# The output projection's last pair of tiles finished one by one, and 1/rms with the mean's constant inside the square

## The chip, the cores and the metric

The kernel runs on one core of a Trainium2 chip, as one program. The metric is the device time of one execution in microseconds (us). Five engines work beside each other and meet at semaphores: TensorE (PE, matmuls and transposes; its weight loads are shown as PEld), VectorE (DVE), ScalarE (ACT), GpSimd (POOL) and SyncE (SP, which issues most of the DMAs). Each engine works off its own list of instructions in order.

## What is computed

The reference is a trunk of four layers over 512 latent tokens (x) and 256 context tokens (xc), 1024 wide, in float32. Layers 0 and 3 mix tokens with a chunked gated linear attention (GLA), layer 1 with windowed attention, layer 2 with a gated linear recurrence (RG-LRU, 1280 wide). Around each mixer stand a norm ahead, an output projection, a norm behind, and a residual:

```python
def rmsnorm(x, g):
    y = xf * lax.rsqrt(jnp.mean(xf * xf, axis=-1, keepdims=True) + EPS)
    return (y * g).astype(x.dtype)

for i in range(DEPTH):
    shift, scale, gate = jnp.split(s_lat @ w_mod[i] + b_mod[i], 3, axis=-1)
    h = rmsnorm(x, g_pre[i]) * (1.0 + scale[:, None, :]) + shift[:, None, :]
    ...
    y, yc = mixer(h, hc, ...)          # ends with (o * silu(z)) @ w_out
    x = x + gate[:, None, :] * rmsnorm(y, g_post[i])
    if ctx_out:                        # all layers but the last
        xc = xc + gate_c * rmsnorm(yc, g_post[i])
```

In a GLA layer each of the four heads' output has a norm of its own ahead of the gate: `o = merge_heads(rmsnorm(o, g_head))`.

## The kernel before

**Tiling.** Tokens lie in six tiles of 128: 0 to 3 are the latent ones, 4 and 5 the context. A float32 product is made of three passes, with both operands split in a rounded part and a rest (wh and wl for weights, Rh and Rl for the layer's input, transposed). `split` (L266 and L269) makes the two parts of a weight: ACT casts wh, then DVE, or for some parts POOL, subtracts to get wl. Weights come through a few buffers; `convert()` splits the next weight into the buffer of an old one, and so waits for that one's last reader.

**`finish` (L758)** is the output projection of a layer with all that stands behind it. Per token tile tt it has two column halves (ch) of 512, and each is summed over two halves of the contraction (kh). The first column half is done in a loop; the second by the generator `halves`, which takes a list of (kh, tt), does one product (L796, 12 matmuls) per step, and behind each product with kh = 1 runs `take` (ACT: Square of the result with a sum to ssq, L803; DVE: result times gate and weight, L804) and `post` (sum of the two halves' squares on DVE, L810, then 1/rms through `rstd_of`). `residual` (L816) adds to x and stores it, `square` is the next layer's sum of squares (ACT, L621, then `rstd_of`), `scale` multiplies by that 1/rms (L823), `norm` transposes one chunk of 256 columns of a tile pair (PE L638), applies the next layer's scale and shift (ACT L642) and splits into Rh and Rl (DVE L649 and L650). There are four chunks per pair; their results are the input of the next layer's first matmuls (L385 and others).

**Order.** In the three finishes that another layer follows, PE, ACT and DVE run in the order in which the code calls these steps (`manual_schedule`); POOL's order and the DMAs come from the scheduler. In the last part the pairs are (2, 3) for products and (0, 1) for the norm: the code there runs the products of tiles 2 and 3 and between them, as fillers, the norm's four chunks of tiles 0 and 1; then residuals, squares and scales of tiles 2 and 3, then the norm of pair (2, 3). The final finish (layer 3) has no norm behind it: it goes tile by tile.

**`rstd_of` (L611 to L616)** makes 1/rms on POOL: L614 multiplies the sum of squares by 1/n and adds EPS, L615 raises to -1/2. It serves rx (the pre-norm, 24 times), ry (the post-norm, 22 times) and ro (the GLA heads' norm, 20 times, 128x2).

**GLA.** In `chunk` (L1178 on) a pair of token tiles of one head is computed: PE L1188, ACT's squares L1190, DVE's multiplication by g_head L1191, `rstd_of`, DVE's scaling L1194 (two), then a transpose L1201. The scheduler orders these between heads: while the last chunks of one head end, the next head begins with `levels`, whose DVE operations are X (L1043) and then, level by level, X and Y (L1105); ACT copies Y to K (L1090), and PE's L1056 needs K.

Of the kernel before, what the change touches and what calls it, by code (L numbers as in the profile page):

```python
# [77 lines left out]
def body(ctx: ExitStack, tc: tile.TileContext, I, out, layers=(0, 1, 2, 3)):  # L78
# [532 lines left out]
    def rstd_of(pool, ss, n, name):  # L611
        w = ss.shape[1]
        r = pool.tile([P, w], F32, name=name, tag=name, bufs=4)
        G.tensor_scalar(r, ss, 1.0 / n, EPS, op0=ALU.mult, op1=ALU.add)  # L614
        G.tensor_tensor(r, r, nhalf.to_broadcast([P, w]), op=ALU.pow)  # L615
        return r  # L616

    def unit_rstd(pool, x, xn):

        ss = pool.tile([P, 1], F32, name="ssx", tag="ssx", bufs=4)  # L620
        S.activation(xn, x, AF.Square, accum_out=ss)  # L621
        return rstd_of(pool, ss, D, "rx")
# [135 lines left out]
    def finish(i, kc, extra, last, final, xsrc, xdst):  # L758
# [4 lines left out]
        with phase(f"fin{i}", 6, 0) as fp:  # L763
# [37 lines left out]
            def take(ch, tt, ps):  # L801
                c = slice(ch * 512, (ch + 1) * 512)
                S.activation(y[tt][:, c], ps, AF.Square, accum_out=ssq[tt][:, ch : ch + 1])  # L803
                V.tensor_tensor(y[tt][:, c], ps, gpt[:, 1 if tt >= 4 else 0, c], op=ALU.mult)  # L804
# [3 lines left out]
            def post(tt):  # L808
                s1 = fp.tile([P, 1], F32, name="s1", tag="s1", bufs=4)
                V.tensor_reduce(s1, ssq[tt], axis=AX.X, op=ALU.add)  # L810
                rs[tt] = rstd_of(fp, s1, D, "ry")
# [29 lines left out]
            def halves(*parts):  # L841

                ps = {}
                for kh, tt in parts:
                    if tt not in ps:
                        ps[tt] = mxt()
                    product(w[kh], kh, 1, tt, ps[tt])
                    yield
                    if kh:
                        take(1, tt, ps[tt])  # L850
                        post(tt)
# [32 lines left out]
            with tc.manual_schedule(engines={PE.engine, S.engine, V.engine}):  # L884
# [17 lines left out]
                h = halves((0, 2), (0, 3), (1, 2), (1, 3))  # L902
# [13 lines left out]
                step((0, 1), 0)  # L916
                next(h)
                norm((0, 1), 1)
                run(h)
                residual(2)  # L920
                norm((0, 1), 2)
                square(2)
                residual(3)
                norm((0, 1), 3)
                scale(2)
# [11 lines left out]
    def gla(i, a, ctx_out):  # L937
# [3 lines left out]
        with phase(f"gla{i}") as mp:  # L941
# [196 lines left out]
            def outputs(h, X, Y, A, v, tl):  # L1138
# [39 lines left out]
                def chunk(pr):  # L1178
# [10 lines left out]
                    for n in range(2):  # L1189
                        S.activation(on[:, n, :], ps[:, n, :], AF.Square, accum_out=ss[:, n : n + 1])  # L1190
                    V.tensor_tensor(on, ps, gh.unsqueeze(1).to_broadcast([P, 2, GDV]), op=ALU.mult)  # L1191
                    rs = rstd_of(mp, ss, GDV, "ro")
# [571 lines left out]
```

## Time and profile before

| | |
|---|---|
| median of 3 runs | 1525.08 us (1524.38 to 1532.94) |
| profiled execution, its own time | 1530.24 us |
| its span | 1528.5 us |
| mean granted TensorE clock | 0.983 |
| busy: PE | 1449.4 us, 95% |
| busy: DVE | 1013.6 us, 66% |
| busy: ACT | 786.9 us, 51% |
| busy: POOL | 190.5 us, 12% |

The profile page lists busy times over the whole span. Since PE is busy for most of it, the places to read are those where it waits. The three tails of `finish` lie at about 421 to 475, 848 to 897 and 1183 to 1224 us, the final one at the very end; the two GLA layers take the stretches from the start to about 421 and from 1224 to the end. The granted clock is the share of TensorE's full speed (2.4 GHz) that it was given; near 0.5 it ran at 1.2 GHz.

### The profile page before, as it was taken

The numbers are of one execution on the slowest core, as the hardware profiler recorded it, in microseconds if no ns is written. First come the engines' busy times: TensorE is split into PE (matmuls) and PEld (weight loads), VectorE is DVE, ScalarE is ACT, GpSimd is POOL, SyncE is SP. The second block draws the span as 40 slices with busy tenths as digits, with TensorE's granted clock in tenths as the row PEclk, the third lists the DMA queues.
The fourth block names the chain that finished last, engine by engine and source line by source line (L and its number), as shares of the span: only waits on it lengthen the run. The fifth ranks groups of instructions, "written<-read, shape, count | busy, mean of one in ns | idle before, by whom it ended". The sixth has DMA issues, their size and how long they took to land.

```text
span 1528.5 us, 29077 instructions
## 1 busy us (share of the span) xinstructions
PE 1449.4 (95%) x11691; PEld 1213.7 (79%) x11691; DVE 1013.6 (66%) x1913; ACT 786.9 (51%) x1543; POOL 190.5 (12%) x301
## 2 busy tenths in 40 slices
PE   5998899999999899999999999899999889999998
PEld 3877788888877777878888787788878778879886
DVE  5585647576264389787883568988962666766754
ACT  4644353524252357655662477878842555355242
POOL 2211101012122200010000210000011311101111
PEclk8999999999999999999999999999999999999999
DMA  9450514112573632122216624212251352121132
GB/s 304 138 149 18 170 56 143 56 33 70 206 235 128 183 94 70 43 66 56 56 45 226 216 82 150 82 49 70 66 188 50 102 158 88 33 59 56 60 110 84
DMA packets 153046, 162.35 MB, mean 106 GB/s; under 512 B 12418, under 2 KB 141968, under 8 KB 152912
## 3 DMA queue, kind: packets, MB, share of 16 engines
q1 hardware_dynamic: 147456, 146.56, 31.0%
q10 hardware_dynamic: 5456, 13.94, 2.5%
q8 instruction: 92, 1.51, 0.4%
q14 instruction: 42, 0.34, 0.1%
HBM read 138.44 MB, written 11.53 MB: 98 GB/s over the span
## 4 chain that ended last, share of the span: by engine, by line
PE 51%; DVE 10%; ACT 7%; DMA 5%; issue 2%; SPq 1%; POOL 1%; ACTq 0%; DVEq 0%; POOLq 0%
PE mxt L796 15%; PE pjt L395 9%; PE pjt L385 6%; PE pjt L1028 4%; PE mxt L1525 3%; PE mxt L1509 2%; DMA raw<-in_w_mod_dram 2%; PE mxt L524 2%; PE sct L1630 2%; PE mxt L1468 1%; PE mxt L1188 1%; PE mxt L1451 1%; DVE wl L269 1%; ACT wh L266 1%; PE mxt L638 1%
## 5 line engine op out<-in xcount | busy, mean ns | idle before, releaser
L385 PE MATMUL pjt<-Rh,wh 128*128 128x256 f32 (+1 forms) x592 | 198.6, 337 | 7.1 <-DVE Rh L649 4.6
L385 PE MATMUL pjt<-Rl,wh 128*128 128x256 f32 (+1 forms) x592 | 198.1, 336 | 2.1 <-DVE Rl L650 1.8
L385 PE MATMUL pjt<-Rh,wl 128*128 128x256 f32 (+1 forms) x592 | 197.2, 334 | 0.7 <-DVE wl L269 0.7
L269 DVE TENSOR_TENSOR wl<-raw,wh 128x1024 fp32r<-128x1024 f32 x105 | 128.4, 1231 | 56.8 <-ACT wh L266 56.4
L266 ACT CAST wh<-raw 128x1024 fp32r<-128x1024 f32 x118 | 122.0, 1053 | 80.8 <-PE mxt L796 33.0
L395 PE MATMUL pjt<-Rl,wh 128*128 128x512 f32 (+1 forms) x448 | 162.0, 362 | 0.0
L395 PE MATMUL pjt<-Rh,wh 128*128 128x512 f32 (+1 forms) x448 | 161.6, 361 | 0.0
L395 PE MATMUL pjt<-Rh,wl 128*128 128x512 f32 (+1 forms) x448 | 161.3, 360 | 0.0
L796 PE MATMUL mxt<-wh,Rh 128*128 128x512 f32 x352 | 138.9, 395 | 0.0
L796 PE MATMUL mxt<-wh,Rl 128*128 128x512 f32 x352 | 137.6, 391 | 0.8 <-DVE Rl L769 0.8
L796 PE MATMUL mxt<-wl,Rh 128*128 128x512 f32 x352 | 137.2, 390 | 0.0
L385 PEld LDWEIGHTS pjt<-Rh,wh 128*128 128x128 f32 x592 | 112.6, 191 | 19.7 <-DVE Rh L649 5.7
L385 PEld LDWEIGHTS pjt<-Rl,wh 128*128 128x128 f32 x592 | 112.7, 191 | 15.9 <-DVE Rl L650 4.1
L385 PEld LDWEIGHTS pjt<-Rh,wl 128*128 128x128 f32 x592 | 112.7, 191 | 12.5 <-DVE wl L269 1.2
L1028 PE MATMUL pjt<-wh,Rh 128*128 128x256 f32 x384 | 110.8, 289 | 1.9 <-ACT wh L266 1.9
L1028 PE MATMUL pjt<-wl,Rh 128*128 128x256 f32 x384 | 110.3, 287 | 1.1 <-DVE wl L269 1.1
L1028 PE MATMUL pjt<-wh,Rl 128*128 128x256 f32 x384 | 110.2, 287 | 0.0
L1487 ACT ACTIVATE pe<-mxt,mxs 128x256 f32<-128x256 f32 (+2 forms) x128 | 70.7, 556 | 54.0 <-DVE mxs L1479 53.1
L395 PEld LDWEIGHTS pjt<-Rh,wl 128*128 128x128 f32 x448 | 86.0, 192 | 9.2 <-issue 1.9
L395 PEld LDWEIGHTS pjt<-Rh,wh 128*128 128x128 f32 x448 | 86.3, 193 | 8.7 <-issue 1.2
L395 PEld LDWEIGHTS pjt<-Rl,wh 128*128 128x128 f32 x448 | 86.2, 193 | 8.5 <-issue 1.3
L1477 DVE TENSOR_REDUCE mxs<-mxt 128x1 f32<-128x256 f32 (+2 forms) x128 | 65.4, 518 | 24.1 <-PE mxt L1468 10.5
(297 smaller groups left out, 3458.1 us busy)
## 6 DMA issues: line engine op xcount, KB each, us to landing
rawp<-in_w_mod_dram SPq DMA_DIRECT2D x48, 512.0 KB, 5.7
raw<-in_w_mod_dram SPq DMA_DIRECT2D x48, 512.0 KB, 3.7
raw<-in_a_w_in_dram SPq DMA_DIRECT2D x32, 512.0 KB, 3.5
raw<-in_b_w_in_dram SPq DMA_DIRECT2D x20, 512.0 KB, 5.1
raw<-in_c_w_in_dram SPq DMA_DIRECT2D x20, 512.0 KB, 3.7
xd<-x SPq DMA_DIRECT2D x18, 512.0 KB
raw<-in_a_w_out_dram SPq DMA_DIRECT2D x16, 512.0 KB, 3.4
x<-xd ACTq DMA_DIRECT2D x16, 512.0 KB, 8.2
```

The costliest lines, as they stand in the source:

```text
L266: S.copy(h, x)
L269: e.tensor_tensor(l, x, h.bitcast(F32), op=ALU.subtract)
L385: PE.matmul(ps, w[u][:, k, c0 : c0 + P], R[v][:, k, t0 : t0 + n], start=(k == 0 and u + v == 0), stop=(k == KC - 1 and u == 1),)
L395: PE.matmul(ps, w[u][:, k, c0 : c0 + P], R[x][:, k, t0 : t0 + n], start=(k == 0 and u + x == 0), stop=(k == KC - 1 and u == 1),)
L524: PE.matmul(ps[32 * g : 32 * g + 32, 0:256], sT[:, k, :], r2[k // 4][:, k % 4, :], start=(n < 4), stop=(n >= 4), skip_group_check=True,)
L796: PE.matmul(ps, l[:, tt * P : (tt + 1) * P], r, start=(k == 0 and u + v == 0), stop=(k == kc - 1 and u == 1),)
L1028: PE.matmul(ps[:, n, :], R[u][:, k, tt * P : (tt + 1) * P], w[x][:, k, :], start=(k == 0 and u + x == 0), stop=(k == KC - 1 and u == 1),)
L1477: V.tensor_reduce(mxs[:, n : n + 1], u[e][:, :w], axis=AX.X, op=ALU.max)
L1487: S.activation(p[:, o : o + w], u[e][:, :w], AF.Exp, bias=nm, scale=0.125, accum_out=den[:, n : n + 1],)
L1509: PE.transpose(u[e][:, c * P : (c + 1) * P], ps[e][:, m * P : (m + 1) * P], ident)
L1525: PE.matmul(po[64 * e : 64 * e + 64, 0:P], v[:, keys[m], 64 * kv : 64 * kv + 64], pt[:, e, m * P : (m + 1) * P], start=(m == len(keys) - 1 ...
L1630: PE.matmul(ps[:, t0 : t0 + nn], wg[a][:, n, :], x[c][:, p0 : p0 + nn], start=(q == 0), stop=(q == 2),)
```

## The change

There are two parts. **The constants:** `rstd_of` no longer multiplies by 1/n. Instead the Square on ACT gets a scale of n to the power -1/2, so that the sum is already the mean. EPS is added on DVE by an operation of its own for rx and ro; for ry it is added in the operation that sums the two halves (a scalar_tensor_tensor in place of the reduction L810). POOL keeps the power alone, so it has 66 instructions fewer, and DVE 44 more. **The order:** in the finishes with a norm behind them, the products of the last pair run (0, 2), (1, 2), (0, 3), (1, 3) in place of (0, 2), (0, 3), (1, 2), (1, 3); residual, square and scale of tile 2 move ahead, and the norm's last chunks of pair (0, 1) stand ahead of tile 3's residual.

```diff
--- before.py
+++ after.py
@@ -608,18 +608,20 @@
             run(open_bg.pop())
 
 
-    def rstd_of(pool, ss, n, name):
+    def rstd_of(pool, ss, name, eps=True):
+
         w = ss.shape[1]
         r = pool.tile([P, w], F32, name=name, tag=name, bufs=4)
-        G.tensor_scalar(r, ss, 1.0 / n, EPS, op0=ALU.mult, op1=ALU.add)
-        G.tensor_tensor(r, r, nhalf.to_broadcast([P, w]), op=ALU.pow)
+        if eps:
+            V.tensor_scalar(r, ss, EPS, None, op0=ALU.add)
+        G.tensor_tensor(r, r if eps else ss, nhalf.to_broadcast([P, w]), op=ALU.pow)
         return r
 
     def unit_rstd(pool, x, xn):
 
         ss = pool.tile([P, 1], F32, name="ssx", tag="ssx", bufs=4)
-        S.activation(xn, x, AF.Square, accum_out=ss)
-        return rstd_of(pool, ss, D, "rx")
+        S.activation(xn, x, AF.Square, scale=D ** -0.5, accum_out=ss)
+        return rstd_of(pool, ss, "rx")
 
     def unit(pool, x, xn):
 
@@ -800,15 +802,15 @@
 
             def take(ch, tt, ps):
                 c = slice(ch * 512, (ch + 1) * 512)
-                S.activation(y[tt][:, c], ps, AF.Square, accum_out=ssq[tt][:, ch : ch + 1])
+                S.activation(y[tt][:, c], ps, AF.Square, scale=D ** -0.5, accum_out=ssq[tt][:, ch : ch + 1])
                 V.tensor_tensor(y[tt][:, c], ps, gpt[:, 1 if tt >= 4 else 0, c], op=ALU.mult)
 
             rs = {}
 
             def post(tt):
                 s1 = fp.tile([P, 1], F32, name="s1", tag="s1", bufs=4)
-                V.tensor_reduce(s1, ssq[tt], axis=AX.X, op=ALU.add)
-                rs[tt] = rstd_of(fp, s1, D, "ry")
+                V.scalar_tensor_tensor(s1, ssq[tt][:, 0:1], EPS, ssq[tt][:, 1:2], op0=ALU.add, op1=ALU.add)
+                rs[tt] = rstd_of(fp, s1, "ry", False)
 
             def residual(tt, parts=1):
                 for m in range(parts):
@@ -899,7 +901,7 @@
                 next(h, None)
                 step((4, 5), 1)
                 run(h)
-                h = halves((0, 2), (0, 3), (1, 2), (1, 3))
+                h = halves((0, 2), (1, 2), (0, 3), (1, 3))
                 step((4, 5), 2)
                 residual(0)
                 next(h)
@@ -914,15 +916,15 @@
                 convert()
                 next(h)
                 step((0, 1), 0)
+                residual(2)
                 next(h)
                 norm((0, 1), 1)
+                square(2)
                 run(h)
-                residual(2)
                 norm((0, 1), 2)
-                square(2)
+                scale(2)
+                norm((0, 1), 3)
                 residual(3)
-                norm((0, 1), 3)
-                scale(2)
                 square(3)
                 scale(3)
                 begin("ctx")
@@ -1187,9 +1189,9 @@
                         for m, (l, r) in enumerate(tm):
                             PE.matmul(ps[:, n, :], l, r, start=(m == 0), stop=(m == len(tm) - 1))
                     for n in range(2):
-                        S.activation(on[:, n, :], ps[:, n, :], AF.Square, accum_out=ss[:, n : n + 1])
+                        S.activation(on[:, n, :], ps[:, n, :], AF.Square, scale=GDV ** -0.5, accum_out=ss[:, n : n + 1])
                     V.tensor_tensor(on, ps, gh.unsqueeze(1).to_broadcast([P, 2, GDV]), op=ALU.mult)
-                    rs = rstd_of(mp, ss, GDV, "ro")
+                    rs = rstd_of(mp, ss, "ro")
                     for n in range(2):
                         V.tensor_scalar(on[:, n, :], on[:, n, :], rs[:, n : n + 1], None, op0=ALU.mult)
                     return on
```

What this moves is shown at three places. In the rows of after, the lines from L616 on are those of before plus 2 (L1196 is L1194 of before).

First, DVE in layer 3, where one head's last chunks meet the next head's first levels (on is the head's output, ro its 1/rms, X and Y the next head's scaled queries and keys). Before:

```order
L1191 TENSOR_TENSOR on<-mxt,gh 128x512
L1194 TENSOR_SCALAR on<-on,ro 128x256 x2
L1043 TENSOR_TENSOR X<-tmp,q 128x2x512
L1191 TENSOR_TENSOR on<-mxt,gh 128x512
L1194 TENSOR_SCALAR on<-on,ro 128x256 x2
L1105 TENSOR_TENSOR X<-X,tmp 128x256x2
L1105 TENSOR_TENSOR Y<-Y,tmp 128x384x2
```

after:

```order
L1193 TENSOR_TENSOR on<-mxt,gh 128x512
L616 TENSOR_SCALAR ro<-sso 128x2
L1196 TENSOR_SCALAR on<-on,ro 128x256 x2
L1045 TENSOR_TENSOR X<-tmp,q 128x2x512
L1193 TENSOR_TENSOR on<-mxt,gh 128x512
L616 TENSOR_SCALAR ro<-sso 128x2
L1196 TENSOR_SCALAR on<-on,ro 128x256 x2
L1107 TENSOR_TENSOR X<-X,tmp 128x256x2
L1107 TENSOR_TENSOR Y<-Y,tmp 128x384x2
```

The addition of EPS (L616) now stands behind each multiplication by g_head and ahead of the scaling that needs the power. This repeats for each head of both GLA layers.

Second, the tail of layer 1's finish, from the casts of `convert()` on (tiles 4 and 5 are done, so their y hold the norm's chunks: y_9209 and y_9213 before, y_9203 and y_9207 after; tiles 2 and 3 are y_9225 and y_9229 before, y_9219 and y_9223 after). ACT before:

```order
L266 CAST wh<-raw 128x1024 x2
L537 COPY mp<-mxt 128x256
L642 ACTIVATE y_9209<-mxt,modT 128x256 x2
L803 ACTIVATE y_9225,ssq_9226<-mxt 128x512
L642 ACTIVATE y_9213<-mxt,modT 128x256 x2
L803 ACTIVATE y_9229,ssq_9230<-mxt 128x512
L642 ACTIVATE y_9209<-mxt,modT 128x256 x2
L266 CAST wh<-raw 128x1024
L621 ACTIVATE y_9225,ssx<-x_9223 128x1024
L642 ACTIVATE y_9213<-mxt,modT 128x256 x2
L621 ACTIVATE y_9229,ssx<-x_9227 128x1024
L266 CAST wh<-raw 128x1024
```

and after:

```order
L266 CAST wh<-raw 128x1024 x2
L805 ACTIVATE y_9219,ssq_9220<-mxt 128x512
L537 COPY mp<-mxt 128x256
L644 ACTIVATE y_9203<-mxt,modT 128x256 x2
L644 ACTIVATE y_9207<-mxt,modT 128x256 x2
L623 ACTIVATE y_9219,ssx<-x_9217 128x1024
L805 ACTIVATE y_9223,ssq_9224<-mxt 128x512
L644 ACTIVATE y_9203<-mxt,modT 128x256 x2
L644 ACTIVATE y_9207<-mxt,modT 128x256 x2
L266 CAST wh<-raw 128x1024
L623 ACTIVATE y_9223,ssx<-x_9221 128x1024
```

Tile 2's take (the first L803, now L805) stands directly behind the casts, its square ahead of tile 3's take, and both last chunks of the norm ahead of tile 3's square. DVE there, from tile 3's sum on (s_9850 before, s_9846 after), before:

```order
L810 TENSOR_REDUCE s_9850<-ssq_9230 128x1
L816 SCALAR_TENSOR_TENSOR x_9223<-y_9225,ry,x_9223 128x1024
L649 CAST Rh<-y_9209 128x2x256
L269 TENSOR_TENSOR wl<-raw,wh 128x1024
L650 TENSOR_TENSOR Rl<-y_9209,Rh 128x2x256
L816 SCALAR_TENSOR_TENSOR x_9227<-y_9229,ry,x_9227 128x1024
L649 CAST Rh<-y_9213 128x2x256
L650 TENSOR_TENSOR Rl<-y_9213,Rh 128x2x256
L823 TENSOR_SCALAR y_9225<-x_9223,rx 128x1024
L823 TENSOR_SCALAR y_9229<-x_9227,rx 128x1024
```

and after:

```order
L812 SCALAR_TENSOR_TENSOR s_9846<-ssq_9224 128x1
L651 CAST Rh<-y_9203 128x2x256
L652 TENSOR_TENSOR Rl<-y_9203,Rh 128x2x256
L825 TENSOR_SCALAR y_9219<-x_9217,rx 128x1024
L651 CAST Rh<-y_9207 128x2x256
L269 TENSOR_TENSOR wl<-raw,wh 128x1024
L652 TENSOR_TENSOR Rl<-y_9207,Rh 128x2x256
L818 SCALAR_TENSOR_TENSOR x_9221<-y_9223,ry,x_9221 128x1024
L616 TENSOR_SCALAR rx<-ssx 128x1
L825 TENSOR_SCALAR y_9223<-x_9221,rx 128x1024
```

Tile 2's scale and both chunks of the norm, with the L269 between the two halves of the last, now stand ahead of tile 3's residual.

Third, POOL in the tail of layer 0's finish (s_4929 and s_4957 before, s_4882 and s_4959 after, are the sums of tiles 2 and 3). Before:

```order
L614 TENSOR_SCALAR ry<-s_4929 128x1
L615 TENSOR_TENSOR ry<-ry,nhalf 128x1
L614 TENSOR_SCALAR ry<-s_4957 128x1
L615 TENSOR_TENSOR ry<-ry,nhalf 128x1
L269 TENSOR_TENSOR wl<-raw,wh 128x1024
L614 TENSOR_SCALAR rx<-ssx 128x1
L615 TENSOR_TENSOR rx<-rx,nhalf 128x1
L614 TENSOR_SCALAR rx<-ssx 128x1
L615 TENSOR_TENSOR rx<-rx,nhalf 128x1
```

and after:

```order
L617 TENSOR_TENSOR ry<-s_4882,nhalf 128x1
L617 TENSOR_TENSOR rx<-rx,nhalf 128x1
L617 TENSOR_TENSOR ry<-s_4959,nhalf 128x1
L269 TENSOR_TENSOR wl<-raw,wh 128x1024
L617 TENSOR_TENSOR rx<-rx,nhalf 128x1
```

The power for tile 2's rx has moved ahead of tile 3's ry and of POOL's L269, and the power for tile 3's rx stands behind that L269 still.

## Rows read from the trace of the kernel before

**Rows 1.** The page: its first line, and busy time by engine (share, instructions)
```profile
span 1528.5 us, 29077 instructions
...
PE 1449.4 (95%) x11691; PEld 1213.7 (79%) x11691; DVE 1013.6 (66%) x1913; ACT 786.9 (51%) x1543; POOL 190.5 (12%) x301
```

**Rows 2.** PE's waits: line waited for, us in total, times, longest
```profile
PE mxt L524 <- DMA rawp<-in_w_mod_dram: 2.6, 1, 2.6
PE sct L1056 <- ACT K L1090: 6.4, 7, 1.1
PE pjt L385 <- DVE Rh L649: 4.6, 4, 2.0
PE mxt L638 <- DVE y L823: 1.7, 2, 1.0
PE mxt L1201 <- DVE on L1194: 0.4, 1, 0.4
```

**Rows 3.** The timeline, last tile: start, us, line, operation, [idle before <-releaser]
```profile
1522.79 0.14 DVE L810 TENSOR_REDUCE s<-ssq 128x1 f32<-128x2 f32 x1
1523.02 0.19 POOL L614 TENSOR_SCALAR ry<-s 128x1 f32<-128x1 f32 x1 [4.61 <-DVE s L810]
1523.30 0.55 POOL L615 TENSOR_TENSOR ry<-ry,nhalf 128x1 f32<-128x1 f32 x1
```

**Rows 4.** The timeline of a chunk handover in layer 3
```profile
1303.66 0.69 DVE L1191 TENSOR_TENSOR on<-mxt,gh 128x512 f32<-128x512 f32 x1 [2.28 <-ACT on L1190]
1303.99 0.70 POOL L615 TENSOR_TENSOR ro<-ro,nhalf 128x2 f32<-128x2 f32 x1
1304.72 0.62 DVE L1194 TENSOR_SCALAR on<-on,ro 128x256 f32<-128x256 f32 x2 [0.37 <-POOL ro L615]
1306.39 0.69 DVE L1191 TENSOR_TENSOR on<-mxt,gh 128x512 f32<-128x512 f32 x1
1307.35 0.62 DVE L1194 TENSOR_SCALAR on<-on,ro 128x256 f32<-128x256 f32 x2 [0.27 <-POOL ro L615]
1311.00 0.67 PE L1056 MATMUL sct<-X,K 128*32 128x32 f32 x32 [0.91 <-ACT K L1090]
```

**Rows 5.** The timeline of a handover in layer 0, DVE
```profile
226.31 0.69 DVE L1191 TENSOR_TENSOR on<-mxt,gh 128x512 f32<-128x512 f32 x1 [0.76 <-ACT on L1190]
226.92 0.41 DVE L492 SCALAR_TENSOR_TENSOR OG<-OG,gz 128x256 f32<-128x256 f32 x1
229.70 1.76 DVE L1043 TENSOR_TENSOR X<-tmp,q 128x1536 f32<-128x1536 f32 x1 [1.72 <-PE mxt L1188]
```

**Rows 6.** The chain that ended last, layer 1's tail: start, us, what
```profile
871.03 2.95 PE mxt L796 x12
```

**Rows 7.** The timeline of layer 1's tail, ACT and DVE
```profile
871.89 2.00 ACT L266 CAST wh<-raw 128x1024 fp32r<-128x1024 f32 x2
888.81 0.75 DVE L823 TENSOR_SCALAR y<-x,rx 128x1024 f32<-128x1024 f32 x1 [0.71 <-POOL rx L615]
```

**Rows 8.** Groups by line in layer 1's tail: busy us, mean ns, idle
```profile
L816 DVE SCALAR_TENSOR_TENSOR x<-y,ry,x 128x1024 f32<-128x1024 f32 x2 | 2.6, 1277 | 0.0
```

**Rows 9.** The timeline of layer 0's tail: POOL, DVE, PE
```profile
458.53 2.60 POOL L269 TENSOR_TENSOR wl<-raw,wh 128x1024 fp32r<-128x1024 f32 x1
458.80 3.41 DVE L816 SCALAR_TENSOR_TENSOR x<-y,ry,x 128x1024 f32<-128x1024 f32 x1
464.66 0.75 DVE L823 TENSOR_SCALAR y<-x,rx 128x1024 f32<-128x1024 f32 x1 [0.72 <-POOL rx L615]
466.50 1.04 PE L638 MATMUL mxt<-ident,y 128*128 128x128 f32 x4
```

**Rows 10.** The timeline of layer 2's tail, PE
```profile
1216.71 3.46 PE L638 MATMUL mxt<-ident,y 128*128 128x128 f32 x15 [0.70 <-DVE y L823]
```

**Rows 11.** Busy time by stretch: us, each engine busy (x), PEclk, DMA, GB/s
```profile
464.00:467.00 3.00, 3.00 (x23) 1.40 (x22) 1.17 (x4) 0.36 (x1) 0.55 (x1) 0.50 0.46 185
1215.00:1222.00 7.00, 6.30 (x31) 5.92 (x31) 3.96 (x8) 3.85 (x8) 0.79 (x2) 0.52 0.14 47
```

## The prediction

> **What bounds the kernel now.** I read the page's head first: 1528.5 us of span, TensorE (PE) busy for 95% of it [rows 1]. The profiled run took 1530.24 us, 1.7 over its span and 5.2 over the median of 1525.08; the sum below is a difference, and I apply it to the median. With PE at 95% a change can only gain or lose where PE waits, so the second view is PE's list of waits [rows 2]. Four of the rows shown touch this change most. The largest is 6.4 us in seven waits for K, the copy that ScalarE (ACT) makes in a GLA layer from Y, which VectorE (DVE) has scaled. Two belong to the tails of the three projections with a following norm: 4.6 us for Rh of the next layer's input and 1.7 us for the scaled tile y. The last, 0.4 us, is for the head norm's output at the end of layer 0. These waits together are 13.1 us, which is the most that it could take away at full clock. The third view is the timeline at those places, to see which engine ends last there.
>
> **The last tile of the program.** Its chain is the reduction L810, POOL's scale-and-add L614, POOL's power L615, the residual [rows 3]. L614 starts 0.23 after L810's start, L615 0.28 after L614. The change puts EPS into the operation at L810's place and drops L614; that scalar_tensor_tensor is not shown here at 128x1, so its price is bounded by nothing and by a rise from 0.14 to POOL's 0.19, and I take 0.14. **-0.3 us**, certain to be on the path, since nothing follows but two stores.
>
> **The head norm (ro), 20 times.** Here L614 goes off POOL too, but to DVE, as an operation of its own behind L1191. Before, POOL adds EPS while DVE multiplies: L1191 starts at 1303.66, the power at 1303.99 already, and the scale L1194 follows at 1304.72, 1.06 after L1191's start [rows 4]. After, the addition stands behind L1191 in DVE's order (the order rows of layer 3 above). L1191 gives way to the next operation 0.61 after its start [rows 5]; the addition, which no row shows on DVE, is bounded by nothing and by 0.19, the time on POOL [rows 3], and I take 0.15 (L810 on two columns is 0.14); the hop to POOL is 0.09 (0.23 less 0.14), the power 0.70, the hop back 0.03 (1303.99 + 0.70 to 1304.72). That makes 1.58 in place of 1.06, **+0.52**. For the second chunk, where the spacing is 0.96 (1306.39 to 1307.35), it is +0.62. Queued behind L1194 on DVE are the multiplications X and Y of L1105, behind Y ACT's copy K, and behind K PE's L1056, which at 1311.00 had waited 0.91 for it [rows 4]. So both delays add up on the path: 1.1 us for each of three heads in layer 3. The order of PE gives one more values matmul ahead of that wait, so I take 0.9 of it: **+2.7**.
>
> In layer 0 there are three chunks. Before the first L1043 DVE was idle for 1.72 us, waiting for PE [rows 5], which swallows the first two delays (1.0 to 1.2 together). The third stands behind L1043 and is not covered: +0.6 for two heads; in the third head DVE's order has an L490 between L1191 and L1194, which covers part, and I take 0.2 (between nothing and 0.6). With +0.3 at the layer's end, where PE already waits 0.4 for L1194 [rows 2], that is **+1.7**. The GLA layers together: +4.4, between 0 (if PE's extra work covers every delay) and +6 (no cover, every chunk's 0.52 to 0.62).
>
> A rule on which engine should do this speaks for the change, and the rows say otherwise. The Trainium skill, page "GPSIMD Engine Reference", section "4.1 Engine selection", sends elementwise work on a tile to VectorE and advises against GpSimd. By that alone the swap of 0.28 on POOL for 0.24 on DVE would cost the GLA layers nothing, and the sum would be +2.4 in place of +6.8; the spacing of 1.06 contradicts it here, because POOL's addition ran beside L1191 and DVE's cannot.
>
> **The three tails.** The products now go (0,2), (1,2), (0,3), (1,3), so tile 2 can be normed one product sooner, and the norm's chunks of tiles 0 and 1 no longer stand behind tile 3's residual. But the reordering also keeps the first weight half (kh = 0) in use until the third product instead of the second, and convert()'s two casts L266, which write the buffer of that half, must wait for its last reader.
>
> Layer 1: the third product ends at 871.03 + 2.95 = 873.98 [rows 6], the casts started at 871.89 [rows 7], so they move by 2.1. In ACT's order tile 2's take stands behind them and has to wait too, so its earlier product buys nothing. On DVE two L269 wait for the casts, then come tile 2's take, three modT operations, chunk 0 and residual 2. Later another L269 stands between L649 and L650 of chunk 3, waiting for a cast that stands behind chunk 3 on ACT, and the last residual (1.28 each [rows 8]) stands behind it. Walking these queues through with the durations of the tail before, tile 3's L823 starts at about 890.9, where it started at 888.81 [rows 7]. PE had no wait of size there, and has four matmuls of the next layer more to do early, so it now waits: **+2.0** (0 to +2.1).
>
> Layer 0: the last residual took 3.41 in place of 1.28, because POOL ran its L269 for 2.60 from 458.53 [rows 8, 9], and PE waited 2.0 for Rh behind it [rows 2]. After, Rh's last chunk stands ahead of the residual, and that wait goes. But POOL's L269, its cast late by the buffer, becomes ready at about 459.1, ahead of the power for rx3 in POOL's order, and falls on DVE's L650 of chunk 3; the residual behind it ends at about 463.5, L823 starts at 465.6 where it was 464.66, and ends at 466.4. PE came to tile 3's transposes at 466.50 before [rows 9], since the work ahead of them ran at a granted clock of 0.50 [rows 11]. So the idle time moves from ahead of that work to behind it: **0** (-2.5 if L269 misses DVE, +1.7 if the low clock then falls on more matmuls).
>
> Layer 2: the same way, POOL's L269 and the memset stand in other gaps; tile 3's L823 ends at about 1217.4 in place of 1216.7, where PE already waited 0.7 for it [rows 10]: **+0.7** (-1.7 to +0.7).
>
> **The first norm and the squares.** The six rx of the first norm take the same swap. They lie beside the first modulation products, which wait 2.6 us for a weight from DMA [rows 2]; that hides them, and without this cover they would cost up to six times 0.52, 3.1 us. The scale in ACT's squares replaces no instruction and adds none, so I cost it at nothing; it is bounded by the spread of ACT's own rows, which show no price for a scale.
>
> **The sum.** -0.3 + 2.7 + 1.7 + 2.0 + 0 + 0.7 = +6.8, that is 1525.1 + 6.8 = 1531.9 us.
>
> **The rivals.**
> Tails pay (chance 0.2). If POOL's L269 of layers 0 and 2 misses DVE's two-input operations, layer 0 gives -2.5, layer 2 -1.7 and layer 1 still +0.9: with +4.4 and -0.3 the sum is +0.8, 1525.9 us. For it: only two of the tail's DVE operations were hit before. Against: the operations that take both inputs from SBUF are now closer together.
>
> The clock stays up (faster; chance 0.15). After the long idle stretches PE ran at 0.50 in 464 to 467 and at 0.52 in 1215 to 1222 [rows 11]; at full clock the work in them would take half, so 1.5 to 1.7 and 3.4 us were lost. If the earlier chunk 3 and tile 2 keep PE fed so that it never falls, those 5 us come back, and with them the 6.3 us of waits for Rh and y [rows 2]: -11.3, and with the GLA layers' +4.4, the -0.3 and half of layer 1's 2.0 some 1519 us. It decides as soon as the tails save more than the GLA layers' 4.4 and layer 1's 2.0, over 6.4 of those 11.3. Against it: by the queues tile 3's L823 is not earlier in any tail.
>
> More clock lost (slower; chance 0.1). The waits for K grow from 0.91 to near 2, and the idle time that led to the 0.50 stretch was of 2.0 [rows 2, 11]. If the clock falls behind three to six of them, at 1.7 each, 1537 to 1542 us. Against: in layer 3 PE has matmuls between these waits.
>
> The change does nothing in the GLA layers (chance 0.1): PE's extra work hides the ro delay, and +2.4 is left, 1527.5 us.
>
> **Chances.** The forecast itself has 0.45, with its own range of 1529 to 1535. The range that should hold 8 in 10 takes in tails that pay and GLA layers that don't, most of the clock rival and the lower half of the slower one: 1520 to 1538. A measurement of this kernel tells about 1% from no change, 15.3 us; of these cases only the ends of the two clock rivals reach below 1509.8 or above 1540.3, so faster 0.02, the same 0.94, slower 0.04.
>
> **What would show it.** In the new trace: the power for ro starting only after L1191's end and L1194 1.6 after L1191's start (the GLA term); PE's waits for K longer by about 0.9 in layer 3; the casts L266 at 874.0 in layer 1's tail and tile 3's L823 near 891; POOL's L269 of layer 0 beside a DVE operation of over 2 us. The prediction is wrong if L1194 follows L1191 as before, if tile 3's L823 comes 2 us earlier in layers 0 and 2, or if the two stretches at half clock are gone.

## The result, and the profile after

The changed kernel took 1539.64 us in the median (1533.69 to 1616.59, 12 runs), the kernel before, run beside it, 1526.68 (1524.38 to 1533.47, 12 runs). The ratio is 1.0079 with a 95% interval of 1.0063 to 1.0095: **slower by 0.8%, some 12 us** (9.6 to 14.5). The forecast was slower by 6.8 us, with 1538.0 as the upper end of the range. The direction was right, the size was too small, and the time lies above the range. (1616.59 is one execution at a granted clock of 0.844, which the ratio leaves out.)

The page of the changed kernel, its first line and busy times [rows 1]:

```profile
span 1531.9 us, 29031 instructions
...
PE 1445.7 (94%) x11691; PEld 1209.0 (79%) x11691; DVE 1019.5 (67%) x1957; ACT 787.0 (51%) x1543; POOL 167.0 (11%) x235
```

The work is the same but for POOL, 23.5 us and 66 instructions less, and DVE, 5.9 us and 44 instructions more. PE's waits (line waited for, us in total, times, longest), as in [rows 2]:

```profile
PE mxt L1203 <- DVE on L1196: 7.2, 15, 0.7
PE sct L1058 <- ACT K L1092: 6.2, 7, 1.1
PE mxt L640 <- DVE y L825: 4.9, 4, 2.4
PE pjt L385 <- DVE Rl L652: 4.4, 10, 1.8
PE pjt L385 <- DVE Rh L651: 2.3, 1, 2.3
```

The row for K, which the forecast said would grow, is where it was: 6.2 us in 7, after 6.4 in 7. What is new is the first row: PE waits 7.2 us in 15 for the head norm's output, where it was 0.4 in one. The wait for y has gone from 1.7 to 4.9, that for Rh from 4.6 to 2.3, and that for Rl from 1.8 to 4.4 us.

The handover in layer 3 that [rows 4] showed, in the timeline after (start, us, engine, line):

```profile
1302.83 0.69 DVE L1193 TENSOR_TENSOR on<-mxt,gh 128x512 f32<-128x512 f32 x1 [2.27 <-ACT on L1192]
1303.44 0.16 DVE L616 TENSOR_SCALAR ro<-sso 128x2 f32<-128x2 f32 x1
1303.67 0.70 POOL L617 TENSOR_TENSOR ro<-ro,nhalf 128x2 f32<-128x2 f32 x1 [30.85 <-DVE ro L616]
1304.41 0.62 DVE L1196 TENSOR_SCALAR on<-on,ro 128x256 f32<-128x256 f32 x2 [0.82 <-POOL ro L617]
1304.91 0.63 PE L1203 MATMUL mxt<-ident,on 128*128 128x128 f32 x4 [0.55 <-DVE on L1196]
1306.08 0.68 DVE L1193 TENSOR_TENSOR on<-mxt,gh 128x512 f32<-128x512 f32 x1
1307.64 0.61 DVE L1196 TENSOR_SCALAR on<-on,ro 128x256 f32<-128x256 f32 x2 [0.81 <-POOL ro L617]
1308.14 0.63 PE L1203 MATMUL mxt<-ident,on 128*128 128x128 f32 x4 [0.20 <-DVE on L1196]
1311.32 0.73 PE L1058 MATMUL sct<-X,K 128*32 128x32 f32 x32 [0.94 <-ACT K L1092]
```

The addition starts 0.61 after L1193, the power 0.23 later, and L1196 1.58 after L1193: the spacing that was forecast, to the hundredth. The second chunk has 1.56 in place of 0.96. PE now waits for this at its own next instruction, the transposes L1203 of the same chunk, before it ever comes to K.

The last tile [rows 3]: the spacing from the sum to the power is 0.22 in place of 0.51.

```profile
1526.52 0.15 DVE L812 SCALAR_TENSOR_TENSOR s<-ssq 128x1 f32<-128x1 f32 x1
1526.74 0.55 POOL L617 TENSOR_TENSOR ry<-s,nhalf 128x1 f32<-128x1 f32 x1 [4.89 <-DVE s L812]
1527.33 1.42 DVE L818 SCALAR_TENSOR_TENSOR x<-y,ry,x 128x512 f32<-128x512 f32 x2 [0.66 <-POOL ry L617]
```

### Where the time went, stage by stage

All 11691 matmuls are in both programs, so a stage can be priced by how much later the same matmul starts (the shift). One trace of before isn't enough for this. The execution shown ahead of the prediction took 1530.24 us, 1.9 to 3.6 over the median of before in any of these comparisons; a second trace of it (the first experiment below) took 1527.11. The table has the shift gained within each stage, from the traces (us, median over the matmuls at the stage's end, less that at its start):

| stage | forecast | against the second trace | against the one shown before |
|---|---|---|---|
| GLA, layer 0, first handover (140 to 158) | +0.6 | +1.1 | +1.1 |
| GLA, layer 0, the others and the end (222 to 425) | +1.1 | +2.0 | +3.1 |
| tail of layer 0 (to 500) | 0 | +1.3 | -0.7 |
| tail of layer 1 (850 to 900) | +2.0 | +1.9 | +1.9 |
| tail of layer 2 (1185 to 1252) | +0.7 | +1.4 | +1.1 |
| GLA, layer 3 (1294 to the last tile) | +2.7 | +4.5 | +4.6 |
| last tile | -0.3 | -0.3 | -0.3 |
| sum of these | +6.8 | +11.9 | +10.8 |
| all the rest | 0 | -5.3 | -7.4 |

Both sums, 11.9 and 10.8, lie in the measured interval of 9.6 to 14.5. The rest differs by several us from execution to execution, and the traced execution of the changed kernel took 1533.69, the least of its twelve, so the difference of two traces' spans (+6.6 and +3.4) says little here.

Not all rows are equally firm. The steps in the GLA layers are the same against either trace: 1.1, 1.0 and 0.7 us at the three handovers of layer 0 and 0.8 at its end, 1.2, 1.3 and 1.3 at those of layer 3 and 0.7 at its end, 8.1 in all. (The table's 7.6 is less by 0.5 which the second trace itself loses behind the second handover.) Layer 1's tail is as steady. Layer 0's tail has +1.0 by 473, the end of its transposes, against the second trace. Behind layer 2's tail the shift against the second trace falls by 1.2 again at 1255, where that trace waits 1.1 us for a weight's DMA and the changed kernel does not.

### The profile page after: what moved, and what is told of

The parts are those of the page before. It is cut to its first block, busy times and chain, and to the rows that moved or that the text cites. A ratio compares the mean times of both kernels' runs of the same rounds, so it can differ in the third digit from the quotient of the medians.

```text
span 1531.9 us, 29031 instructions
## 1 busy us (share of the span) xinstructions
PE 1445.7 (94%) x11691; PEld 1209.0 (79%) x11691; DVE 1019.5 (67%) x1957; ACT 787.0 (51%) x1543; POOL 167.0 (11%) x235
## 4 chain that ended last, share of the span: by engine, by line
PE 48%; DVE 13%; ACT 7%; DMA 4%; issue 3%; POOL 1%; SPq 1%; ACTq 0%; DVEq 0%; POOLq 0%
PE mxt L798 14%; PE pjt L395 9%; PE pjt L385 6%; PE pjt L1030 4%; PE mxt L1527 2%; PE mxt L1511 2%; PE sct L1632 2%; DVE wl L269 1%; PE mxt L1470 1%; PE mxt L524 1%; ACT wh L266 1%; PE mxt L1453 1%; DMA raw<-in_w_mod_dram 1%; DMA bb<-in_b_mod_dram 1%; PE mxt L1162 1%
## 5 line engine op out<-in xcount | busy, mean ns | idle before, releaser
L269 DVE TENSOR_TENSOR wl<-raw,wh 128x1024 fp32r<-128x1024 f32 x105 | 128.0, 1230 | 56.5 <-ACT wh L266 56.0
L806 DVE TENSOR_TENSOR y<-mxt,gpt 128x512 f32<-128x512 f32 x44 | 30.3, 689 | 75.6 <-ACT y L805 75.4
```

Of the source, the lines that this page charges most:

```text
L269: e.tensor_tensor(l, x, h.bitcast(F32), op=ALU.subtract)
```

## The experiments

### A second trace of the kernel before

No edit.

> The kernel before once more, for a second trace of it. The profiled execution shown of it took 1530.24 us, 2 to 3.5 over its median, and shows stretches at half clock at 464 and 536 us and none near 1290, where the changed kernel and all four variants have one. Theory A (which stretches fall to half clock differs from execution to execution; the tail of layer 0 is about 1 us slower with the change than with an undisturbed clock): the new trace lacks the stretch at 464 or 536 or both, or has the one near 1290. Rival E (those stretches belong to the kernel): the same stretches again.

1527.11 us. Busy time by stretch in layer 0's tail (stretch, its length, then PE, PEld, DVE, ACT, POOL busy in us with counts, PEclk, DMA share, GB/s), and near 1290:

```profile
464.00:467.00 3.00, 3.00 (x34) 2.13 (x33) 1.40 (x5) 0.95 (x3) 0.85 (x2) 1.00 0.59 228
1288.00:1291.00 3.00, 3.00 (x12) 2.66 (x11) 2.43 (x4) 0.58 (x2) 0.00 (x0) 0.51 0.66 193
```

PE's first transposes of tile 3 in layer 0's tail, in the timeline:

```profile
465.65 0.68 PE L638 MATMUL mxt<-ident,y 128*128 128x128 f32 x4
```

The clock is 1.00 here, where the trace shown had 0.50 in 464 to 467 [rows 11], and PE comes to the transposes without a wait, 29.1 us after the pair's first product in place of 30.7 [rows 9]. The stretch near 1290, which the shown trace lacks, is there in this one, at 0.50. Theory A holds: those stretches belong to an execution, not to the kernel. Over all fourteen traces, the stretch near 464 stands in four: in the one shown and in three of the variants below.

### The two halves of the change apart

The first has the diff's hunk in the order of the finish alone, with `rstd_of` and its callers as before:

> The order of the finish as in the change, the constants as before (POOL does L614 and L615 for rx, ry and ro). Theory A (most of the loss is the head norm's EPS behind L1191 on DVE, about 7 us by the shift of PE's matmuls between the two traces; the tails cost about 2): +1 to +4 us, 1528 to 1531, PE's waits for the head norm's output near the 0.4 us of before. Rival B (the loss comes from the tails, the constants cost nothing): +9 to +13, 1536 to 1540. Rival C (a lower granted clock in more runs, from either part): the time tells nothing apart, but the mean granted clock of the runs lies under that of before's.

1535.18 us against 1528.31, ratio 1.0046 (1.0028 to 1.0064), +4 to +10. PE's wait for the head norm's output is back at 0.4, the shift in its GLA layers grows by no more than 0.1 at any handover, and the tails' shifts in its trace are +2.5, +2.0 and +1.4. (Of the +2.5, 1.1 stands by 473; the rest lies behind the tail, where PE waits 2.7 us for a weight's DMA in place of 1.3.) That is more than theory A allowed for and less than rival B. Rival C falls: the mean granted clock of the runs is 0.985, as that of before's.

The second has the other hunks, the constants, with the order as before:

> The constants as in the change, the order of the finish as before. Theory A: +6 to +9 us, 1533 to 1536, with PE's waits for the head norm's output near the 7.2 us in 15 waits of the changed kernel. Rival B: within 2 us of before.

1537.14 us, ratio 1.0055 (1.0035 to 1.0075), +5 to +11, about 8 in the middle, as theory A said; PE waits 7.3 us in 15 for the head norm's output, and its trace has the steps of the changed kernel, 1.1 to 0.7 us, at every handover. Both halves cost: about 8 us for the constants, 4 to 7 for the order (the 12 of the whole less 8, and the 7 measured alone).

### The head norm: the place in the queue, not the operation

```diff
-                    V.tensor_tensor(on, ps, gh.unsqueeze(1).to_broadcast([P, 2, GDV]), op=ALU.mult)
                     rs = rstd_of(mp, ss, "ro")
+                    V.tensor_tensor(on, ps, gh.unsqueeze(1).to_broadcast([P, 2, GDV]), op=ALU.mult)
```

> The changed kernel with one line moved: the head norm's addition of EPS is written, and stands in DVE's order, ahead of the multiplication by g_head (L1191 of before) and not behind it. As many instructions as the changed kernel. Theory A (it is the place in DVE's queue that costs, not the operation): the scaling follows about 1.0 after the addition's start, as before the change, PE's waits for the head norm's output fall from 7.2 to under 1 us, and the time lies 6 to 8 us under the changed kernel: 1528 to 1533. Rival D (the addition itself, 20 times on DVE, or POOL's power beside DVE's multiplication, is what costs): no more than 3 us are won, 1535 to 1539.

1535.61 us, ratio 1.0036 (1.0019 to 1.0054); by the medians alone, 1535.61 over 1528.31, it would be 1.0048. The timeline of the same handover:

```profile
1306.32 0.17 DVE L616 TENSOR_SCALAR ro<-sso 128x2 f32<-128x2 f32 x1 [2.30 <-ACT on L1192]
1306.40 0.69 DVE L1194 TENSOR_TENSOR on<-mxt,gh 128x512 f32<-128x512 f32 x1
1306.57 0.70 POOL L617 TENSOR_TENSOR ro<-ro,nhalf 128x2 f32<-128x2 f32 x1 [30.27 <-DVE ro L616]
1307.31 0.62 DVE L1196 TENSOR_SCALAR on<-on,ro 128x256 f32<-128x256 f32 x2 [0.22 <-POOL ro L617]
1307.81 0.63 PE L1203 MATMUL mxt<-ident,on 128*128 128x128 f32 x4
```

The addition now lies ahead of the multiplication, POOL's power beside it, and L1196 follows 0.99 after the addition's start. PE has no wait for the head norm's output left. Layer 0's four steps of 1.1 to 0.7 us are gone; in layer 3 the three handovers keep 0.4 us each in place of 1.2 to 1.3. The same number of operations, one line apart, so it is the place that costs nearly all of it. By the ratios it lies 6.6 us under the changed kernel (0.0043 of 1527), as theory A said, though not under 1533; rival D's "no more than 3 us are won" falls. And with EPS on POOL for ro alone:

```diff
-            V.tensor_scalar(r, ss, EPS, None, op0=ALU.add)
+            (E or V).tensor_scalar(r, ss, EPS, None, op0=ALU.add)
...
-                    rs = rstd_of(mp, ss, "ro")
+                    rs = rstd_of(mp, ss, "ro", E=G)
```

> The changed kernel, but the head norm's EPS is added on POOL, as a tensor_scalar of the same form as before; rx and ry as in the change. Theory A: as the run with the addition ahead, 1529 to 1534, at most 2 us slower than it, since POOL's addition ends 0.1 to 0.2 us later than DVE's. Rival D: faster than the run with the addition ahead by 2 to 3 us, since DVE has 20 operations fewer.

1532.92 us, ratio 1.0037 (1.0019 to 1.0055), the wait at 0.4 in one. By the ratios it is level with the run with the addition ahead; by the medians it is 2.7 us faster, and each ratio is good to some 2.7 us only. So the times don't decide what the 20 short operations on DVE cost. The traces bound it: the steps here are 0.1 us or less at every handover, so the run with the addition ahead keeps some 0.3 at each of layer 3's three, about 1 us, that this one doesn't. So much of rival D may be right.

### The tails: four edits to the order

All four are made to the changed kernel. The first:

```diff
-                h = halves((0, 2), (1, 2), (0, 3), (1, 3))
+                h = halves((0, 2), (0, 3), (1, 2), (1, 3))
...
-                residual(2)
                 next(h)
+                residual(2)
                 norm((0, 1), 1)
```

> The changed kernel with the products of the last pair in the order before, (0,2), (0,3), (1,2), (1,3), and tile 2's residual one step later; the norm's last chunks still ahead of tile 3's residual. Theory A (layer 1's tail is late because the casts wait for the first weight half and stand ahead of tile 2's take): the casts there start 2.1 us earlier, layer 1's tail costs 0 to 1 us in place of 2, 1535 to 1539 (the head norm's 7.5 stays). Rival F (it is late because chunk 3 of the norm, with an L269, stands ahead of tile 3's residual on DVE): layer 1's tail stays 1.5 to 2 us late, 1537 to 1541.

1542.88 us, ratio 1.0080 (1.0057 to 1.0104; six runs of 1535.98 to 1545.50). The second:

```diff
                 norm((0, 1), 2)
+                residual(3)
                 scale(2)
                 norm((0, 1), 3)
-                residual(3)
                 square(3)
```

> The changed kernel with tile 3's residual put ahead of tile 2's scale and of the norm's last chunk; the products tile by tile as in the change. Theory A (the casts): layer 1's tail stays 1.5 to 2 us late, 1537 to 1541. Rival F (what stands ahead of the residual): tile 3's scale in layer 1's tail comes 2 to 3 us earlier than in the changed kernel, and the time lies 3 to 6 us under it, 1533 to 1537.

1539.33 us, ratio 1.0071 (1.0051 to 1.0092). The third:

```diff
-                convert()
                 next(h)
                 step((0, 1), 0)
                 residual(2)
+                convert()
                 next(h)
```

> The changed kernel with convert() behind tile 2's residual, so that its two casts on ACT and two L269 on DVE stand behind tile 2's take and residual and not ahead. Theory G (in layer 1's tail the casts, which wait for the third product, hold up tile 2's take, so that tile 2's square falls ahead of tile 3's take): tile 2's take comes 4 us earlier, tile 3's take 1 to 2 us earlier, tile 3's transposes start 27 to 28 us after the pair's first product in place of 29.4 (27.3 before): 1534 to 1538. Rival F (only what stands between tile 3's take and its scale counts): they start within 0.5 us of 29.4, and the time stays as that of the changed kernel.

1538.69 us, ratio 1.0067 (1.0039 to 1.0095). The fourth:

```diff
-                square(2)
                 run(h)
+                square(2)
                 norm((0, 1), 2)
```

> The changed kernel with tile 2's square behind the fourth product, so that on ACT tile 3's take stands ahead of it. Theory H (tile 3 is late because tile 2's square, 1.06 us, and the residual that it waits for stand ahead of tile 3's take on ACT): in layer 1's tail tile 3's take on DVE comes 1 to 1.6 us earlier and its transposes as much, 28 us after the pair's first product: 1536 to 1539. Rival F: the take comes earlier, but DVE's chunks still stand ahead of the residual, and the transposes stay at 29 to 29.5.

1540.70 us, ratio 1.0086 (1.0056 to 1.0115). None of the four can be told from the changed kernel by its time. Their traces of layer 1's tail can be told apart; the table gives starts in us after the pair's first product (L796), from each trace:

| | first cast | take 2 on DVE | take 3 on DVE | residual 3 | scale 3 | transposes of tile 3 |
|---|---|---|---|---|---|---|
| before, both traces | 9.7 | 15.7 | 18.9 | 22.9 | 26.6 | 27.3 |
| changed | 11.8 | 15.2 | 20.5 | 25.2 | 28.6 | 29.4 |
| products as before | 9.7 | 15.7 | 20.3 | 25.0 | 28.4 | 29.2 |
| residual 3 first | 11.8 | 15.2 | 20.5 | 22.5 | 27.3 | 28.6 |
| convert() behind | 14.5 | 11.5 | 20.3 | 23.8 | 27.2 | 28.0 |
| square 2 behind | 11.8 | 15.2 | 19.7 | 24.6 | 28.0 | 28.8 |
| all mended (below) | 14.5 | 11.2 | 20.3 | 22.0 | 25.8 | 27.1 |

With the products as before the casts start at 9.7 again, and the tail is still 1.9 late: the wait for the first weight half is not the cause by itself. Moving the casts behind tile 2's take brings that take 3.7 us forward, as theory G said, but tile 3's take by 0.2 only; there the theory fails, though the transposes come at 28.0, the edge of its 27 to 28. The gain of 1.4 comes further on: the L269 that stood between chunk 3's L651 and L652 has slipped behind the residual in DVE's order, and the residual comes sooner. Square 2 behind tile 3's take is worth 0.6 (theory H wanted 1 to 1.6). Residual 3 ahead of chunk 3 brings scale 3 forward by 1.3 (rival F wanted 2 to 3) and the transposes by 0.8. No single place holds the 2.1 us. DVE is busy for 12.65 of 14 us of this tail in the changed kernel, where it was for 11.01 in the same stretch of before (second trace, first line; the columns are as above, DVE behind PE and PEld):

```profile
870.00:884.00 14.00, 13.91 (x114) 12.70 (x114) 11.01 (x21) 9.20 (x19) 4.69 (x8) 1.00 0.48 169
871.00:885.00 14.00, 14.00 (x114) 12.84 (x114) 12.65 (x22) 8.61 (x19) 1.81 (x3) 1.00 0.35 112
```

and the change puts tile 2's residual ahead of tile 3's take and scale 2, chunk 3 and an L269 ahead of residual 3. Which of these places holds how much is not shown further than by these four edits.

### All of it mended, and the constants kept where they cost nothing

The second and third of these edits together, and in `rstd_of` (for rx and ro alike):

```diff
-            V.tensor_scalar(r, ss, EPS, None, op0=ALU.add)
+            G.tensor_scalar(r, ss, EPS, None, op0=ALU.add)
```

> Three edits to the changed kernel together: EPS of rx and ro on POOL, convert() behind tile 2's residual, tile 3's residual ahead of tile 2's scale and of the norm's last chunk. If these are the places that cost, the head norm's 7.5 us and the tails' 4 to 5 us go, and layer 1's and layer 2's tails are shorter than before by 1 to 2 us each: 1523 to 1528. If the tails are bound by the sum of DVE's work in them, whatever its order: 1528 to 1531.

1528.93 us against 1527.82, ratio 1.0006 (0.9985 to 1.0027), -2 to +4 us. As far as that tells, the whole loss is gone and nothing is won. That lies in the second range of the expectation; that the tails are bound by the sum of DVE's work is not shown by it. By its trace against the second one of before, the steps in the GLA layers are 0.1 or less, and the tails' shifts are +0.2 (to 473), +0.8 and, in layer 2, -0.4 by 1240. PE's transposes of tile 3 in layer 1's tail, and the first product that they are counted from:

```profile
862.53 0.48 PE L798 MATMUL mxt<-wh,Rh 128*128 128x512 f32 x1
888.30 0.75 DVE L825 TENSOR_SCALAR y<-x,rx 128x1024 f32<-128x1024 f32 x1 [0.77 <-POOL rx L617]
889.60 0.66 PE L640 MATMUL mxt<-ident,y 128*128 128x128 f32 x4
```

The scale is ready at 888.30 + 0.75 = 889.05, and PE comes to the transposes at 889.60 with no wait ahead of them. In layer 1 PE was never short of work in this tail before the change either, so a tile that is ready sooner finds PE still at other matmuls. In layer 0 the scale starts 1.7 us sooner than in the second trace of before, but falls on POOL's L269 there and takes 2.84 us in place of 0.75 (rows in the last section). In between, with residual 3 first and EPS on POOL but `convert()` where it was:

> The same with EPS added on POOL for rx and ro, so that only ry loses an instruction. By both parts of the explanation the head norm's 7.5 us go, and if rival F holds the tails are won too: 1525 to 1529, level with the kernel before or up to 3 us faster. If the casts hold the tails up: 1529 to 1533.

1534.39 us, ratio 1.0031 (1.0013 to 1.0049), above both of the expected ranges. The head norm's part is won by its trace (0.1 at each handover); only the place of `convert()` lies between it and the run above, and the intervals overlap. At last the second kernel of the halves, the constants with the old order, with that edit in `rstd_of`, so that only ry has one POOL instruction less:

> The kernel before with the mean's constant in the squares and EPS of ry in the sum of the two halves, but EPS of rx and ro added on POOL, and the order of the finish as before. If the head norm's EPS on DVE and the order of the tails are the whole loss, nothing of it is left: 0 to -2 us against the kernel before. If moving the constant into the square costs something by itself: +2 us or more.

1527.92 us, ratio 0.9997 (0.9979 to 1.0014). The constant in the square and the shorter ry cost nothing and save nothing that can be measured. No version beats the kernel before.

## Why the prediction was right or wrong, step by step

**Right: the delay itself in the GLA layers.** EPS behind L1191 makes 1.06 into 1.58, as forecast, and 0.94 to 1.39 into 1.56 or 1.57; it does so in 19 of the 20 chunks. In the very last the spacing goes from 1.25 to 2.76, and there PE doesn't wait. **Wrong: where it lands, and so its size**, the term of +4.4 that measured +8.1 by the steps. The step that failed is the path. The forecast carried the delays on to the wait for K, in layer 3 at 0.9 a head, and in layer 0 let DVE's idle 1.72 us ahead of L1043 swallow the first two of each head. PE's own transposes of the same chunk stand earlier in PE's queue, and they were left out: [rows 2] has a wait for them in one place only, of 0.4. That was no room. In the trace of before shown first, the transposes of the chunks of [rows 4] start without a listed wait, 0.50 after L1194's first half started:

```profile
1305.22 0.63 PE L1201 MATMUL mxt<-ident,on 128*128 128x128 f32 x4
1307.85 0.63 PE L1201 MATMUL mxt<-ident,on 128*128 128x128 f32 x4
```

After, they start 0.50 after L1196 again, now with a wait: PE had come to them just as their input was ready (0.04 us before the first of these two, in the trace of before). With EPS on POOL PE waits there once, with EPS behind L1191 15 times. So the delay is paid chunk by chunk, and K finds PE already late. In layer 3 a handover costs 1.2 to 1.3, not 0.9, and the last head, which the sum left out, 0.7 more. In layer 0 each of the four places costs 0.4 to 0.5 more than forecast, which is the first chunk's 0.52: PE waits 0.54 to 0.56 for it in each head. The idle time covers the second chunk alone, whose transposes start some 2 us behind L1194 before and after. The deduction for one more values matmul isn't to be seen in the shifts. Of layer 3's 4.5, 2.8 us stand in PE's waits for L1196; the rest no row of waits names. The term's upper bound of +6, called "every chunk's 0.52 to 0.62", was wrong as a sum too: twenty chunks at that price would be 10.4 to 12.4.

**Wrong: layer 0's tail, 0 forecast and +1.0 to +1.3 measured.** What would happen on POOL and DVE was right: L269 falls on the second half of chunk 3.

```profile
460.20 2.48 POOL L269 TENSOR_TENSOR wl<-raw,wh 128x1024 fp32r<-128x1024 f32 x1 [1.06 <-ACT wh L266]
460.50 2.74 DVE L652 TENSOR_TENSOR Rl<-y,Rh 128x512 fp32r<-128x512 f32 x1
463.29 0.39 PE L385 MATMUL pjt<-Rl,wh 128*128 128x256 f32 x1 [1.80 <-DVE Rl L652]
466.53 0.76 DVE L825 TENSOR_SCALAR y<-x,rx 128x1024 f32<-128x1024 f32 x1 [0.73 <-POOL rx L617]
467.34 0.55 PE L640 MATMUL mxt<-ident,y 128*128 128x128 f32 x3 [0.41 <-DVE y L825]
```

L652 takes 2.74 beside it. Two steps failed. The forecast said of the 2.0 for Rh that "that wait goes". Rh is there in time, but PE needs Rl of the same chunk as well, and waits 1.80 for L652. That is the longest wait of the new Rl row. And L825 starts 29.6 us after the pair's first product, where it was 28.9 and 28.4 in the two traces of before; the forecast offset this by PE's arrival at 466.50, which came from a stretch at half clock [rows 9, 11] that the second trace doesn't have. PE is there 1.6 us sooner, and the transposes come 1.3 later than in that trace. The forecast cancelled a delay against a row of one execution. With the constants alone, in the old order, the shift of this tail by 473 is -0.1, with the order alone +1.1: it is the order's.

**Right in size, wrong in cause: layer 1's tail.** Tile 3's L825 was forecast 2.1 later, and is 2.0 later (28.6 in place of 26.6). The rows:

```profile
870.00 1.99 ACT L266 CAST wh<-raw 128x1024 fp32r<-128x1024 f32 x2 [2.08 <-issue]
871.90 0.59 ACT L805 ACTIVATE y<-mxt 128x512 f32<-128x512 f32 x1
...
883.36 1.27 DVE L818 SCALAR_TENSOR_TENSOR x<-y,ry,x 128x1024 f32<-128x1024 f32 x1
886.73 0.75 DVE L825 TENSOR_SCALAR y<-x,rx 128x1024 f32<-128x1024 f32 x1 [0.73 <-POOL rx L617]
887.54 0.55 PE L640 MATMUL mxt<-ident,y 128*128 128x128 f32 x3 [1.24 <-DVE y L825]
```

The casts start when the third product ends, as forecast, and PE waits 1.24. But with the casts back in their place the tail stays late, so that step of the forecast alone is not what makes it so; the L269 and the chunk ahead of the residual, which it named second, are a part of it.

**Right in kind, too small: layer 2's tail**, +0.7 forecast and +1.1 to +1.4 measured; PE waits there for L825. POOL's L269 fell on a DVE operation here too, the cast L651 of the norm's last chunk, which takes 2.57 in place of 0.42; PE's one wait for Rh, 2.3 us, is for it:

```profile
1206.94 2.77 POOL L269 TENSOR_TENSOR wl<-raw,wh 128x1024 fp32r<-128x1024 f32 x1 [0.42 <-ACT wh L266]
1207.43 2.57 DVE L651 CAST Rh<-y 128x512 fp32r<-128x512 f32 x1
1214.02 0.75 DVE L825 TENSOR_SCALAR y<-x,rx 128x1024 f32<-128x1024 f32 x1 [0.73 <-POOL rx L617]
1214.83 3.16 PE L640 MATMUL mxt<-ident,y 128*128 128x128 f32 x15 [2.40 <-DVE y L825]
```

**The last tile's -0.3** holds. So does the nothing for the first norm: by 60 us the shift against the second trace is -0.7, with the constants alone -0.1. **The rivals:** tails that pay need L269 to miss DVE in layers 0 and 2, and it missed in neither. A clock that stays up: the changed kernel's trace has no stretch at 0.50 near 464, and layer 2's tail has 0.57 over 1210 to 1218, as before in kind; but the first was an accident of the trace shown, so there was nothing to win back. In the second trace PE waits as long in front of it (1.96 at 462.91) and runs on at 1.00, so that idle time alone, which the rival of more clock lost built on, doesn't tell where the clock falls. No new stretches at half clock behind the GLA waits appeared either: the one near 1289 is in the second trace of before too. The rule on engine choice in the Trainium skill, page "GPSIMD Engine Reference", section "4.1 Engine selection", by which the GLA term would be nothing, doesn't hold here: the constants alone bring 7.3 us of waits.

**The median.** The sum was set on a median of three runs, 1525.08; with 12 runs it is 1526.68, which by itself is 1.6 of the 7.7 us between the forecast and the time. The GLA term is 3.7 more of it, layer 0's tail 1.0 to 1.3, layer 2's 0.4 to 0.7.

## What to carry to other kernels

Where two short steps run beside a long one on another engine, moving one of them to the engine with the long one puts it behind that one: look at what stands ahead of it in the queue before counting its own time. A consumer with no wait in the profile may have no slack (time to spare) either; compare its start with its input's end before a delay is passed on to a later wait. Before a delay is cancelled against idle time or a slow clock, look at a second execution: both may belong to the one that was profiled.

## What the runs showed of the hardware

The granted clock fell to 0.50 at different places in executions of the same kernel: at 464, 536 and 658 us in one trace of before, at none of these in the other, which has a stretch at 1288 that the first lacks. In the five traces with such a stretch between 534 and 546 us (attention, which no edit touches), the shift against the second trace of before grew there by 2.8 to 3.9 us, in the eight others by -0.7 to +0.9. The Trainium skill, page "SBUF — State Buffer", section "🔬 SBUF: two separate sides", calls the pair of ports that DVE and POOL share an exclusive lock, held for a whole instruction; the 2.74 us of L652 beside POOL's 2.48 agrees: it ends 0.56 us after POOL's, close to the 0.69 that it takes alone. Operations with one tensor input are held up as well: the cast above took 2.57 in place of 0.42, and with all mended L825 took 2.84 beside POOL's 2.36 of L269, where it takes 0.75 alone.

```profile
463.21 2.36 POOL L269 TENSOR_TENSOR wl<-raw,wh 128x1024 fp32r<-128x1024 f32 x1
463.27 2.84 DVE L825 TENSOR_SCALAR y<-x,rx 128x1024 f32<-128x1024 f32 x1 [0.77 <-POOL rx L617]
```
